# The modulation's accumulation steps moved from the neighbourhood projections to the queries, latent keys and values

## The chip, the cores and the metric

The kernel runs on one core of a Trainium2 chip. The metric is the device time in microseconds (us), the median of several executions. Five engines work side by side on queues of their own: TensorE (PE: matrix products into PSUM), VectorE (DVE), ScalarE (ACT), GpSimd (POOL) and SyncE (SP, which here issues the DMA loads). An instruction waits at the head of its engine's queue until what it needs is there, and everything queued behind it waits too.

## The reference, cut to what matters

One step of a diffusion backbone with two layers. In each layer 128 context tokens and 256 latent tokens (384 in three tiles of 128) go through a half-step feed-forward block, a block of three token mixers on the same input, and a second feed-forward block:

```
m  = split(silu(cvec) @ w_ada[l] + b_ada[l], 9)      # modulation, once for c_ctx and once for c
xp = ffn(modulate(xp, m[0], m[1]), gate m[2])
u_f, u_q, u_kv, k_rope, u_na = split(modulate(xp, m[3], m[4]) @ w_in)
y_f = fourier(u_f) @ w_branch_f
y_m = attention(query(u_q), keys and values of the latent kv) @ w_branch_m
y_n = neighbourhood_attention(q, k, v of u_na) @ w_branch_n
xp = xp + m[5] * ((sigmoid(h @ w_gate) * (y_f, y_m, y_n)) @ w_out)
xp = ffn(modulate(xp, m[6], m[7]), gate m[8])
```

The modulation is `silu(cvec) @ w_ada`: for each layer a matrix of 1024 x 9216 in fp32, read for two vectors only.

## The kernel before

All matrix products are fp32 values split into a high and a low part, three matmuls for one product: PE writes a result to one of eight PSUM banks, ACT writes the high part from the bank (a CAST), and DVE subtracts it for the low part (a TENSOR_TENSOR). The bank is free for a new result when both have read it. All PSUM tiles are taken from one pool in turn, so a new tile reuses the bank of the tile eight places earlier. Weights are split in the same way when loaded (`raw` into `whi` by ACT, `wlo` by DVE).

The modulation's matrix is not multiplied on PE. It is accumulated on DVE, a step at a time (`ada_step`): a step loads 128 rows x 1024 columns of `w_ada` (512 KB) and adds them, times one scalar per partition, to two accumulators `acc`, one for each vector. These are two SCALAR_TENSOR_TENSOR instructions; the first step of a block of eight has two TENSOR_SCALAR instead. After eight steps `ada_finish` transposes both accumulators (STREAM_TRANSPOSE, `at`) and reduces them (`red`), four DVE instructions more; three flushes later `ada_place` has one small matmul (`ada`, which takes a PSUM bank) and four small DVE instructions (`mod`), or for a gate block a write to DRAM.

Steps are issued by `ada_spend(n)` (L497), which takes n steps from the stage's budget, flushes what is due, and stops at a budget of zero:

```
budget = {(0, 0): 36, (0, 1): 12, (0, 2): 36, (1, 0): 36, (1, 1): 8, (1, 2): 0}
```

So layer 0's mixers spend 12 steps and layer 1's 8. In `mixer_body` the order of the code is: transposed queries and Fourier mixing, `query(t)` three times (tile `q`, `qtok`), the latent keys in four pairs (PSUM tile `kn`, results `k`), the latent values in four tiles (`v`, `vs`), the transposed heads (`qT`, `q`), eight chunks of the Fourier branch (`yb`, copied by DVE to `mg`), the latent attention, in whose fill the neighbourhood's values are projected (`nv`), then the neighbourhood's queries and keys (`nq`, `nk`, eight chunks), its attention, and the last branch. Before the change the steps stand with `nv` (three), ahead of `nq` (one) and with the `nq`/`nk` chunks (up to eight).

The order on PE, DVE and ACT is set by a scheduler from the order of the code and the dependences; SP keeps the order of the code. Loads are placed by a planner (`make_plan`, `place`), which gives each weight its moment from a clock of PE work and the free slots among 26 large buffers.

Of the kernel before, what the change touches and what calls it, by code (L numbers as in the profile page):

```python
# [88 lines left out]
class Kernel:  # L89
# [879 lines left out]
    def mixer_body(self, ph):  # L969
# [61 lines left out]
            ckT.append(kt)  # L1031

        def query(t):
            c = slice(t * P, (t + 1) * P)
            qk = self.slot([P, NH, HQ], F32, "qtok")
            for hh in range(2):
                b = self.psum("q")
                for kc in range(3):
                    w = self.W(("wuq", l, kc), "mla_w_uq", l, kc * P, 1, 0, 768)
                    self.mm3(b[:, 0:384], (qnT[kc][:, 0, c], qnT[kc][:, 1, c]),  # L1040
                             tuple(x[:, 0, hh * 384:hh * 384 + 384] for x in w), kc == 0, kc == 2)
                bv = b[:, 0:384].rearrange("p (h j) -> p h j", h=4)
                qs = qk[:, 4 * hh:4 * hh + 4]
                if t == 0:
                    nc.scalar.copy(out=qs, in_=bv)
                else:
                    nc.scalar.copy(out=qs[:, :, 0:64], in_=bv[:, :, 0:64])
                    self.rope(qs[:, :, 64:96], bv[:, :, 64:96], t - 1, 4)
            qtok.append(qk)

        for step, i in ((turn_q, 0), (turn_q, 1), (turn_q, 2), (four_tokens, 0), (four_tokens, 1), (four_tokens, 2), (four_tokens, 3),
                        (four_channels, 0), (turn_kv, 0), (turn_kv, 1), (query, 0), (four_channels, 1), (query, 1), (query, 2)):
            step(i)
# [7 lines left out]
        k96 = [self.slot([HQ, 2, 512], F32R, "k96") for _ in range(NH)]  # L1061
        w = self.ukv(l, 0)
        for pr in range(4):
            b = self.psum("kn")
            for kc in range(2):
                lhs = tuple(x[:, kc, 2 * pr:2 * pr + 2].rearrange("p a b -> p (a b)") for x in w)
                self.mm3(b, lhs, (ckT[kc][:, 0], ckT[kc][:, 1]), kc == 0, kc == 1)
            for e in range(2):
                kk = k96[2 * pr + e]
                self.split(kk[0:64, 0], kk[0:64, 1], b[64 * e:64 * e + 64, :])  # L1070
                nc.vector.tensor_copy(out=kk[64:96], in_=krt[64:96].bitcast(F32))
        w = self.ukv(l, 1)
        vm = []
        for t in range(4):
            b = self.psum("v")
            for kc in range(2):
                self.mm3(b, (ckT[kc][:, 0, t * P:(t + 1) * P], ckT[kc][:, 1, t * P:(t + 1) * P]),
                         tuple(x[:, kc].rearrange("p a b -> p (a b)") for x in w), kc == 0, kc == 1)
            vm.append(self.split_v(b))
# [494 lines left out]
```

## Time and profile before

| what | us |
|---|---|
| median of three runs | 1869.28 (1868.36 to 1870.4) |
| profiled execution | 1866.74 |
| its span, first to last instruction | 1865.0 |
| PE busy in it | 1842.9 |
| DVE busy in it | 1409.0 |

The profiled execution has its own time, 2.5 us under the median; stretches are read from it, and a change found in it is set on the median. Stretches are told in us from the span's start. Layer 0's queries, keys, values and Fourier branch lie between 353 and 395, its `nq` and `nk` between 471 and 506; layer 1's between 1273 and 1315 and between 1392 and 1426. An engine's idle time is shown in brackets with what ended it.

### The profile page before, as it was taken

What the parts mean: (1) busy time and instruction counts of PE and PEld (TensorE: products, weight loads), DVE (VectorE), ACT (ScalarE), POOL (GpSimd) and SP (SyncE); (2) the same over time, 40 slices, a digit from 0 to 9 for tenths busy, and PEclk for the clock granted to TensorE, in tenths of its full rate; (3) what the DMA queues carried; (4) which work ended last, traced back from release to release, by engine and by line L of the source; (5) the groups of instructions that cost most, each with busy time, mean ns of one, the idle gap of its engine ahead of it and who ended that gap; (6) DMA issues with size and microseconds to landing.
All of it is one profiled execution on the core that took longest, in us unless ns stands there. A gap on an engine that the chain in (4) does not pass through costs nothing. (4 is left out here: it accounts for less than half of the span.)

```text
span 1865.0 us, 27258 instructions
## 1 busy us (share of the span) xinstructions
PE 1842.9 (99%) x10568; PEld 1728.1 (93%) x10568; DVE 1409.0 (76%) x2206; ACT 785.3 (42%) x1305; POOL 94.7 (5%) x115
## 2 busy tenths in 40 slices
PE   8999999999999999999999999999999999999998
PEld 6899998999899999999999999989999998999997
DVE  6788888689997677888876888978798776533345
ACT  4433335556355453332453333355554553533330
POOL 0000002000100010000000000120001000000000
PEclk9999999999999999999999999999999999999999
DMA  9766656234835446666545666542356353444522
GB/s 325 264 224 212 206 209 207 88 102 126 234 109 188 125 148 221 196 226 219 188 159 186 221 220 219 193 157 89 113 177 183 104 190 130 133 135 125 145 92 79
DMA packets 225602, 320.22 MB, mean 172 GB/s; under 512 B 32784, under 2 KB 181888, under 8 KB 225344
## 3 DMA queue, kind: packets, MB, share of 16 engines
q1 hardware_dynamic: 223328, 313.88, 52.5%
q0 software_dynamic: 2112, 4.59, 0.6%
q8 instruction: 83, 1.36, 0.3%
q14 instruction: 47, 0.39, 0.1%
q10 hardware_dynamic: 32, 0.01, 0.0%
HBM read 312.32 MB, written 8.02 MB: 172 GB/s over the span
## 5 line engine op out<-in xcount | busy, mean ns | idle before, releaser
L193 DVE TENSOR_TENSOR wlo<-raw,whi 128x1024 fp32r<-128x1024 f32 (+4 forms) x420 | 488.7, 1181 | 148.7 <-ACT whi L188 68.0
L188 ACT CAST whi<-raw 128x1024 fp32r<-128x1024 f32 (+4 forms) x420 | 420.3, 1020 | 325.9 <-DVE wlo L193 83.7
L77 PE MATMUL w<-hmh,whi 128*128 128x384 f32 x1152 | 388.3, 337 | 0.8 <-ACT sl L77 0.8
L77 PE MATMUL w<-hmh,wlo 128*128 128x384 f32 x1152 | 387.1, 336 | 0.0
L77 PE MATMUL w<-hml,whi 128*128 128x384 f32 x1152 | 387.1, 336 | 0.0
L77 PE MATMUL y<-whi,sT 128*128 128x512 f32 x1050 | 335.1, 391 | 1.7 <-DVE sT L77 1.5
L77 DVE SCALAR_TENSOR_TENSOR acc<-raw,cs,acc 128x1024 f32<-128x1024 f32 x236 | 296.9, 1290 | 28.8 <-DMA raw<-in_w_ada_dram 28.5
L77 PEld LDWEIGHTS y<-whi,sT 128*128 128x128 f32 x1050 | 196.8, 188 | 41.1 <-DVE sT L77 2.1
L77 PEld LDWEIGHTS w<-hmh,whi 128*128 128x128 f32 x1152 | 216.6, 188 | 3.2 <-ACT sl L77 1.1
L77 PEld LDWEIGHTS w<-hml,whi 128*128 128x128 f32 x1152 | 216.6, 188 | 1.9
L77 PEld LDWEIGHTS w<-hmh,wlo 128*128 128x128 f32 x1152 | 216.6, 188 | 0.0
L77 PE MATMUL y<-wlo,sT 128*128 128x512 f32 x525 | 204.2, 389 | 0.0
L77 PE MATMUL g<-hmh,whi 128*128 128x384 f32 x384 | 132.5, 345 | 1.4 <-DVE qN L77 1.4
L77 PE MATMUL g<-hmh,wlo 128*128 128x384 f32 x384 | 129.8, 338 | 1.6 <-DVE wlo L193 1.6
L77 PE MATMUL g<-hml,whi 128*128 128x384 f32 x384 | 129.9, 338 | 0.0
L77 PEld LDWEIGHTS y<-wlo,sT 128*128 128x128 f32 x525 | 98.6, 188 | 18.1
L77 ACT CAST sT<-sl 128x384 fp32r<-128x384 f32 x72 | 37.1, 515 | 183.8 <-DVE sl L77 183.8
L77 PE MATMUL hd<-whi,hmh 128*128 128x256 f32 (+1 forms) x336 | 100.1, 300 | 1.6 <-ACT hmh L77 1.6
L77 PE MATMUL hd<-wlo,hmh 128*128 128x256 f32 (+1 forms) x336 | 99.0, 297 | 0.0
L77 PE MATMUL hd<-whi,hml 128*128 128x256 f32 (+1 forms) x336 | 98.9, 296 | 0.0
L77 ACT ACTIVATE sl<-w 128x384 f32<-128x384 f32 x72 | 35.4, 492 | 110.0 <-PE w L77 109.7
L77 POOL TENSOR_TENSOR st<-st,mhalf 128x1 f32<-128x1 f32 x48 | 43.9, 916 | 689.3 <-DVE st L77 689.2
(271 smaller groups left out, 2952.3 us busy)
## 6 DMA issues: line engine op xcount, KB each, us to landing
raw<-in_ffn_w_dram SPq DMA_DIRECT2D x244, 512.0 KB, 5.0
raw<-in_w_ada_dram SPq DMA_DIRECT2D x128, 512.0 KB, 4.9
raw<-in_w_gate_dram SPq DMA_DIRECT2D x48, 512.0 KB, 4.1
raw<-in_w_in_dram SPq DMA_DIRECT2D x32, 512.0 KB, 6.1
raw<-in_w_ada_dram SPq DMA_DIRECT2D x32, 256.0 KB, 5.9
raw<-in_w_out_dram SPq DMA_DIRECT2D x16, 512.0 KB, 6.8
raw<-gd SPq DMA_DIRECT2D x12, 512.0 KB, 5.1
raw<-in_ffn_w_dram SPq DMA_DIRECT2D x22, 256.0 KB, 5.8
```

Of the source, the lines that this page charges most:

```text
L77: r = f(*a, **kw)
L188: self.real.scalar.copy(out=hi, in_=r)
L193: self.real.vector.tensor_tensor(out=lo, in0=r, in1=hi.bitcast(F32), op=ALU.subtract)
```

## The change

Three lines are added in `mixer_body`: one step ahead of each of the three query tiles, one ahead of each of the four pairs of keys, and one ahead of every second of the four value tiles. The budgets stay, so each step spent here is one that the later calls no longer have.

```
         def query(t):
+            self.ada_spend(1)
             c = slice(t * P, (t + 1) * P)
...
         for pr in range(4):
+            self.ada_spend(1)
             b = self.psum("kn")
...
         for t in range(4):
+            self.ada_spend(t % 2)
             b = self.psum("v")
```

In layer 0 nine of the twelve steps are spent by these lines and three with `nv`; none is left for `nq` and `nk`. In layer 1 all eight are spent here. The accumulator's block ends inside the moved steps in both layers: in layer 0 with the first step of the keys, in layer 1 with the last step, at the values.

On DVE in layer 0, at the first two pairs of keys (`kn` is the pair's bank, `k` the split keys, `krt` the rotary part that is copied in). Before:

```order
L77 TENSOR_TENSOR k_648_3489<-kn_3497,k_648_3489 64x512
L77 CAST k_648_3489<-krt_3486 32x1024
L77 CAST k_649_3490<-krt_3486 32x1024
L77 TENSOR_TENSOR k_649_3490<-kn_3497,k_649_3490 64x512
L77 TENSOR_TENSOR k_650_3491<-kn_3512,k_650_3491 64x512
```

and now:

```order
L77 SCALAR_TENSOR_TENSOR acc_2385<-raw_3265,cs_161,acc_2385 128x1024
L77 TENSOR_TENSOR k_654_3507<-kn_3517,k_654_3507 64x512
L77 CAST k_654_3507<-krt_3504 32x1024
L77 CAST k_655_3508<-krt_3504 32x1024
L77 TENSOR_TENSOR k_655_3508<-kn_3517,k_655_3508 64x512
L77 STREAM_TRANSPOSE at_3531<-acc_2384 128x1024
L77 STREAM_TRANSPOSE at_3534<-acc_2385 128x1024
L77 TENSOR_REDUCE red_3530<-at_3531 128x32
L77 TENSOR_REDUCE red_3530<-at_3534 128x32
L77 TENSOR_SCALAR acc_3537<-raw_3292,cs_161 128x1024
L77 TENSOR_SCALAR acc_3538<-raw_3292,cs_161 128x1024
L77 TENSOR_TENSOR k_656_3509<-kn_3543,k_656_3509 64x512
```

Between the first pair's keys and the second's stand the end of one block and the first step of the next. Eight `acc` instructions (four steps) stand on DVE ahead of the first pair in both layers: two steps between the split of the last `uq` weights and the low part of `f`, the third among the transposed queries and the Fourier products, and the two halves of the fourth ahead of the second Fourier chunk and ahead of the first key. Behind that, layer 0 has a step after the second and after the third pair, and one behind the first and one behind the third value tile; layer 1 has a step after each of the first three pairs, one behind the first value tile, and the block's end behind the second.

On PE in layer 0, where the last pair of keys gives way to the first value tile. Before:

```order
L77 MATMUL kn_3542<-ckT_3348,whi_3310 128x512 x2
L77 MATMUL kn_3542<-ckT_3348,wlo_3311 128x512
L77 MATMUL v_3555<-whi_3397,ckT_3338 128x512
L77 MATMUL v_3555<-wlo_3398,ckT_3338 128x512
L77 MATMUL v_3555<-whi_3397,ckT_3348 128x512
```

and now:

```order
L77 MATMUL kn_3579<-ckT_3360,whi_3322 128x512 x2
L77 MATMUL kn_3579<-ckT_3360,wlo_3323 128x512
L77 MATMUL ada_3594<-red_3530,quad_105 128x64
L77 MATMUL v_3601<-whi_3415,ckT_3352 128x512
L77 MATMUL v_3601<-wlo_3416,ckT_3352 128x512
```

The small matmul on `red` stands in front of the values and takes a bank, so that the tiles behind it reuse banks one place earlier: the first `yb` chunk has the bank of the fourth pair of keys, where before it had the third's.

On DVE in layer 0, at the first `nq` and `nk` chunks. Before:

```order
L77 SCALAR_TENSOR_TENSOR acc_4668<-raw_4583,cs_161,acc_4668 128x1024
L77 SCALAR_TENSOR_TENSOR acc_4669<-raw_4583,cs_161,acc_4669 128x1024
L193 TENSOR_TENSOR wlo_4709<-raw_4619,whi_4708 128x1024
L193 TENSOR_TENSOR wlo_4727<-raw_4621,whi_4726 128x1024
L77 TENSOR_TENSOR kN_4739<-nk_4704,kN_4739 128x384
L77 TENSOR_TENSOR kN_4739<-cnkT_4655,kN_4739 128x128
L77 COPY kf_4660<-nk_4704 128x128
L77 SCALAR_TENSOR_TENSOR acc_4668<-raw_4593,cs_161,acc_4668 128x1024
L77 SCALAR_TENSOR_TENSOR acc_4669<-raw_4593,cs_161,acc_4669 128x1024
```

and now:

```order
L77 SCALAR_TENSOR_TENSOR qN_4739<-nq_4714,qN_4739 128x384
L193 TENSOR_TENSOR wlo_4747<-raw_4641,whi_4746 128x1024
L193 TENSOR_TENSOR wlo_4765<-raw_4644,whi_4764 128x1024
L77 TENSOR_TENSOR kN_4779<-cnkT_4708,kN_4779 128x128
L77 TENSOR_TENSOR mod_3596<-ada_4785,bad_107 32x16 x3
L77 TENSOR_TENSOR kN_4779<-nk_4742,kN_4779 128x384
L77 COPY kf_4713<-nk_4742 128x128
```

No `acc` instruction is left there; the end of the second block stands just ahead of these rows.

## Rows read from the trace of the kernel before

**Rows 1.** The page's first part: engine, busy us (share of the span), instructions.

```profile
PE 1842.9 (99%) x10568; PEld 1728.1 (93%) x10568; DVE 1409.0 (76%) x2206; ACT 785.3 (42%) x1305; POOL 94.7 (5%) x115
```

**Rows 2.** Stretches: length, then busy PE, PEld, DVE, ACT, POOL; PE clock, DMA share, GB/s.

```profile
353.00:365.00 12.00, 12.00 (x74) 11.96 (x73) 11.38 (x35) 8.22 (x17) 0.00 (x0) 1.00 0.00 1
365.00:376.00 11.00, 11.00 (x52) 9.17 (x51) 9.99 (x22) 5.64 (x10) 0.00 (x0) 1.00 0.00 1
376.00:392.00 16.00, 15.57 (x90) 14.88 (x90) 14.62 (x22) 8.79 (x13) 0.00 (x0) 1.00 0.34 104
392.00:440.00 48.00, 48.00 (x316) 47.81 (x315) 37.93 (x85) 29.32 (x71) 0.00 (x0) 1.00 0.29 87
...
510.00:515.00 5.00, 4.18 (x15) 4.18 (x16) 5.00 (x7) 0.27 (x1) 2.48 (x1) 0.66 0.26 85
...
1426.00:1515.00 89.00, 89.00 (x590) 88.14 (x587) 67.83 (x174) 50.67 (x109) 2.43 (x2) 1.00 0.42 137
```

**Rows 3.** Waits of PE in the mixers: total us, times, longest us.

```profile
PE yb L77 <- DVE k L77: 0.4, 1, 0.4
...
PE g L77 <- DVE wlo L193: 1.6, 1, 1.6
PE g L77 <- DVE qN L77: 1.4, 1, 1.4
```

**Rows 4.** Timeline of PE in layer 0: start, us, instruction [idle before, releaser].

```profile
380.06 0.59 PE L77 MATMUL yb<-oF,whi 128*128 128x384 f32 x2 [0.43 <-DVE k L77]
```

**Rows 5.** Timeline of DVE in layer 0, from the last kv norm to the values.

```profile
344.74 0.48 DVE L77 SCALAR_TENSOR_TENSOR ckv<-kv,st,raw 128x256 f32<-128x256 f32 x1 [0.73 <-POOL st L77]
...
348.31 0.69 DVE L77 TENSOR_TENSOR f<-uf,f 128x512 fp32r<-128x512 f32 x1 [2.60 <-ACT f L77]
...
351.35 0.57 DVE L77 TENSOR_TENSOR gl<-fa,gh 128x392 fp32r<-128x392 f32 x1 [0.48 <-ACT gh L77]
...
365.75 0.29 DVE L77 TENSOR_TENSOR qtok<-q,rp 128x128 f32<-128x128 f32 x1 [0.62 <-ACT qtok L77]
...
379.22 0.69 DVE L77 TENSOR_TENSOR k<-kn,k 64x512 fp32r<-64x512 f32 x1
...
381.69 1.88 DVE L77 TENSOR_TENSOR vs<-v,vs 128x512 fp32r<-128x512 f32 x3
```

**Rows 6.** Timeline of DVE in layer 0, at the first `nk` chunk: a block's end and steps.

```profile
479.63 1.21 DVE L77 TENSOR_REDUCE red<-at 128x32 f32<-128x1024 f32 x1
480.76 1.24 DVE L77 STREAM_TRANSPOSE at<-acc 128x1024 f32<-128x1024 f32 x1
481.92 0.71 DVE L77 TENSOR_SCALAR acc<-raw,cs 128x1024 f32<-128x1024 f32 x1
...
484.33 2.48 DVE L77 SCALAR_TENSOR_TENSOR acc<-raw,cs,acc 128x1024 f32<-128x1024 f32 x2
486.73 2.35 DVE L193 TENSOR_TENSOR wlo<-raw,whi 128x1024 fp32r<-128x1024 f32 x2
```

**Rows 7.** The chain that ended last, layer 1: start, us, engine and what.

```profile
1299.28 0.68 DVE k L77
...
1300.10 14.80 PE yb L77 x84
```

**Rows 8.** Timeline of DVE in layer 1, the second to fourth value tiles.

```profile
1301.72 1.88 DVE L77 TENSOR_TENSOR vs<-v,vs 128x512 fp32r<-128x512 f32 x3
```

**Rows 9.** Timeline of PE in layer 0, behind the neighbourhood's first scores.

```profile
510.82 0.45 PE L77 MATMUL g<-hmh,wlo 128*128 128x384 f32 x1 [1.64 <-DVE wlo L193]
...
511.31 0.52 PE L77 MATMUL g<-hml,whi 128*128 128x384 f32 x1
...
514.20 0.52 PE L77 MATMUL g<-hml,whi 128*128 128x384 f32 x1
```

**Rows 10.** The page's DMA issues: count, KB each, median us from issue to landing.

```profile
raw<-in_w_ada_dram SPq DMA_DIRECT2D x128, 512.0 KB, 4.9
```

More of the change, by code (lines that the diff above doesn't have):

```diff
@@ L1033, in query @@
         def query(t):
+            self.ada_spend(1)
             c = slice(t * P, (t + 1) * P)
@@ L1063, in mixer_body @@
         for pr in range(4):
+            self.ada_spend(1)
             b = self.psum("kn")
@@ L1074, in mixer_body @@
         for t in range(4):
+            self.ada_spend(t % 2)
             b = self.psum("v")
```

## The prediction

> **What bounds the kernel now.** I read the page's first part, then stretches of the mixers, then PE's waits, then the timelines. Over the whole span PE is busy 99% and DVE 76% [rows 1], which looks as if DVE had room everywhere. The stretches say otherwise. Where the steps go, DVE is the fuller engine: 11.38 of 12 us, 9.99 of 11 and 14.62 of 16 from 353 to 392 [rows 2]. PE still shows no idle time there because it runs ahead of DVE on its eight banks. How much of that lead is left is shown by the one wait in this stage: the second `yb` chunk waits 0.4 us for DVE's last keys, in layer 0 at 380.06 (the same row stands once more in layer 1) [rows 3, 4]. The lead is used up. Whatever delays DVE's keys now delays PE by as much.
>
> The Trainium skill (Perfetto Trace Analysis, Identifying the Most-Contended Engine) ranks engines by occupancy. By that ranking over the span, PE alone binds, DVE work is free, and the result is the third rival's. The same page (Optimization Strategy) lets the contended engine change with the regime; the stretches and the 0.4 us wait agree with that half.
>
> Where the steps came from, PE loses something in layer 0 alone. Its first gate chunk behind the scores waits 1.4 us for DVE's `qN` and 1.6 us for a `wlo` [rows 3], and after that the granted clock is 0.66 in a stretch of 5 us [rows 2]: ten matmuls start 0.32 us apart from 511.31 to 514.20 [rows 9] against 14.80 us for 84, 0.176 each, at the full 2.4 GHz [rows 7]. Ten times 0.145 is 1.4 us. In layer 1 PE is busy in every microsecond from 1426 to 1515 [rows 2].
>
> **The change, part by part.**
>
> *Removed.* Layer 0's `nq`/`nk` lose nine steps' worth of DVE time, so I take all three losses as gone: 1.4 + 1.6 + 1.4 = 4.4 us. The block's end that still stands there (four instructions) is hidden under chunks on which PE never waited before. Layer 1 gains nothing, since PE had no wait there.
>
> *Prices on DVE.* Two SCALAR_TENSOR_TENSOR in a row hold DVE from 484.33 to 486.73: a step costs 2.40 us, an instruction 1.20. A transpose takes 480.76 to 481.92, 1.16, and a reduction 479.63 to 480.76, 1.13; a block's end is two of each, 4.58. From 481.92 to 484.33 are two TENSOR_SCALAR and one reduction, so a block's first step is 2.41 - 1.13 = 1.28 [rows 6].
>
> *Added ahead of the first keys, both layers.* Eight `acc` instructions, 9.60 us. What absorbs them is DVE's idle time in that stretch: 0.73 before `ckv` and 2.60 before the low part of `f`, then five short waits for ACT from 0.48 (at 351.35) to 0.62 (at 365.75), 2.22 together [rows 5]. That is 5.55. ACT and POOL, on which these waits hung, keep their times, so a later DVE finds them done. DVE reaches the first keys 9.60 - 5.55 = 4.05 us late. The same order stands in layer 1, with the same idle times to 0.1 us, so I use 4.05 twice.
>
> *Layer 0 from there.* The block's end, 4.58, a first step, 1.28, and two steps, 4.80, come before the last keys: 4.05 + 4.58 + 1.28 + 4.80 = 14.7 us late. The last keys ended at 379.22 + 0.69 = 379.9 [rows 5], now 394.6. Because the `ada` matmul took a bank, the first `yb` chunk waits for exactly these keys. From 394.7 eight chunks take 8/7 of 14.80, 16.9 us, to 411.6; before, seven of them ran from 380.06 [rows 4] to 394.9. PE is 16.8 us late. The two steps among the values do not add to this: the second value tile ends at about 382.3 + 14.7 + 3.1 (a step and the small `mod` instructions) = 400.1 against 401.0, when PE comes to the chunk that takes its bank, and the fourth at 383.6 + 14.7 + 5.5 = 403.8 against 405.3 [rows 5].
>
> *Layer 1.* Three steps lie between the first and the last keys: 4.05 + 7.20 = 11.3, so the second `yb` chunk starts at 1311.4 instead of 1300.1 [rows 7]. One more step and the block's end come before the third value tile, which ended at 1303.0 (two thirds through 1.88 us from 1301.72 [rows 8]) and now ends 4.05 + 9.60 + 4.58 = 18.2 later, at 1321.2. The fifth chunk takes its bank; four chunks, 8.4 us, end at 1329.6, against 1314.9 before [rows 7]. PE is 14.7 us late.
>
> *Is it given back?* DVE's lag is worked off under `yb`, but PE's is not: it is busy 48.00 of 48 us from 392 to 440 [rows 2], so nothing behind the delay can shrink.
>
> *Clock.* Each layer now has long waits of PE among the keys and values. Before, 3.0 us of waits were followed by a half-speed stretch that cost 1.4 [rows 9]. Inside the stretch that DVE sets, slow matmuls cost nothing; behind the last wait they do. I take 1.4 once a layer, 2.8, between 0 and one drop for each of three long waits a layer, 8.4.
>
> *Loads.* Nine loads of `w_ada` now stand in SP's queue among those of `w_ukv` and `w_branch_f` and ahead of `w_gate`. DMA is idle from 353 to 376 (share 0.00) [rows 2], a load lands in 4.9 us [rows 10], and most of the new ones only wait for buffers that PE frees in the `uq`, `kv` and `uf` projections. I cost them at nothing; if that cover fails, DVE waits one landing in each layer, 9.8 us.
>
> *Sum.* 16.8 + 14.7 - 4.4 + 2.8 = 29.9 us. The profiled execution, 1866.74, becomes 1896.6; the median, 1869.28, becomes 1899.2, which is the forecast.
>
> **The rivals.**
>
> *The clock keeps dropping.* PE's work in the two stages falls into short bursts between waits, and the half speed reaches into chunks that PE sets. For it: the drop came after only two waits [rows 9]. Against it: only the last burst of each layer lies on the path. Six drops of 1.4 instead of two: 1904.8. The Trainium skill (TensorE: Matmul & The Clock Gate, A second HAM failure mode: psum-queue depth-cycling) describes a kernel whose small waits while cycling through banks sent the clock back and forth at a cost in throughput. By that account this rival holds; the trace has one drop and cannot decide.
>
> *Loads come late.* One landing more in each layer, 9.8 us: 1909.0. For it: branch and gate weights now wait for buffers that the moved steps release, so their loads start later. Against it: the empty DMA before.
>
> *DVE has room after all.* The steps hide behind PE, and only the gain is left: 1869.28 - 4.4 = 1864.9. It decides if PE's lead on the banks, measured where `yb` begins, is larger than the 15 us by which DVE falls back; the wait there says that the lead is 0. For it speaks only the 76% over the span.
>
> *A draw.* The lead covers all but some 4 us, which the gain cancels: 1869.3. It needs the same hidden lead.
>
> That the change does not do what it says is excluded by the order: no `acc` row is left in the projections.
>
> **How the numbers follow.** Forecast 0.66, clock 0.14, late loads 0.12, room on DVE 0.05, draw 0.03. The forecast's own lower bound is no clock loss, -2.8, and as much idle absorbed again as I counted, -11.1: 1885. Its upper bound, no idle absorbed, +11.1, gives 1910, and the late loads end at 1909. I take 1885 to 1911; outside lie the two cases around no change, 0.08, and some of the combined mishaps. A measurement of this kernel can tell about 0.2%, 3.7 us, from no change. Faster 0.05, same 0.03, slower 0.92.
>
> **What would show it.** In the changed profile PE should wait for DVE in layer 0 at the `ada` matmul, at a `qT` transpose and at the first `yb` chunk, some 17 us together, and in layer 1 at the transposes, the first two `yb` chunks and the fifth, some 15; DVE should be busy without a gap from `f` to the Fourier branch; the clock should fall below 1 near 395 and 1321; the `g` waits of 1.4 and 1.6 should be gone; `acc` should never wait for its load. The forecast is wrong if PE's idle time in the two stages is under 10 us, if DVE shows gaps there that end on a DMA, or if layer 0's `g` waits stay.

## The result, and the profile after

The changed kernel takes 1895.49 us (median of 4 runs, 1893.84 to 1895.88) against 1868.82 for the kernel before in the same session: a ratio of 1.0142, 95% interval 1.0124 to 1.0159, so 26.5 us slower (23.2 to 29.7). The forecast was 1899.2 in a range of 1885 to 1911. The profiled execution took 1895.4 us, its span 1893.6.

The page after, for [rows 1]: busy time, then the PE clock in 40 slices of the span.

```profile
PE 1851.7 (98%) x10568; PEld 1734.4 (92%) x10568; DVE 1405.3 (74%) x2206; ACT 784.9 (41%) x1305; POOL 94.3 (5%) x115
...
PEclk8999999989999999999999999998999999999999
```

The two 8s behind the start are the slices with the two mixers' key and value stages. The stretches there, to be read against [rows 2]: length, then busy PE, PEld, DVE, ACT, POOL, the PE clock, the DMA share, GB/s.

```profile
353.00:365.00 12.00, 11.69 (x77) 11.39 (x77) 12.00 (x23) 8.29 (x15) 0.00 (x0) 1.00 0.47 180
365.00:376.00 11.00, 9.88 (x51) 8.52 (x50) 10.86 (x36) 4.54 (x10) 0.00 (x0) 1.00 0.07 23
376.00:412.00 36.00, 24.33 (x108) 22.20 (x109) 34.97 (x46) 11.43 (x17) 0.00 (x0) 0.81 0.25 75
412.00:460.00 48.00, 48.00 (x317) 47.81 (x316) 38.38 (x86) 29.12 (x71) 0.00 (x0) 1.00 0.37 111
520.00:540.00 20.00, 20.00 (x124) 19.68 (x124) 12.98 (x37) 9.14 (x21) 0.00 (x0) 1.00 0.45 127
```

DVE fills every stretch up to 412 and PE stands for 11.7 of 36 us. From 520 to 540, where the neighbourhood's first scores and gate chunks lie now, PE is busy throughout at full clock; before, it waited for `qN` and `wlo` at this place, 508 to 511 [rows 3, 9].

Waits of PE after, in layer 0 from 335 to 420: total us, times, longest us.

```profile
PE ada L77 <- DVE red L77: 6.2, 1, 6.2
PE yb L77 <- DVE k L77: 4.6, 1, 4.6
PE qT L77 <- DVE k L77: 2.0, 1, 2.0
PE fa L77 <- DVE f L77: 0.7, 1, 0.7
PE fo L77 <- DVE gl L77: 0.3, 1, 0.3
```

And in layer 1, from 1250 to 1350:

```profile
PE yb L77 <- DVE k L77: 6.7, 2, 5.8
PE yb L77 <- DVE vs L77: 1.7, 1, 1.7
PE qT L77 <- DVE k L77: 1.1, 1, 1.1
...
```

Every one is on DVE, none on a load, and DVE itself waits for no load in these stages. The places are those that the prediction named, and two that it did not: `fa` and `fo` wait for DVE's part of `f` and `gl`, which is late too (0.7 and 0.3 us in each layer).

To add up layers and kernels I use marks on PE's timeline: the first `fa` matmul, where the Fourier branch begins, the first score `s` behind the `yb` chunks, and the first `nq` of layer 0. First the kernel before, then the changed one; columns are start, us, instruction.

```profile
348.40 0.36 PE L77 MATMUL fa<-whi,f 128*128 128x260 f32 x1
...
394.72 1.50 PE L77 MATMUL s<-k,q 96*128 96x384 f32 x9
...
471.86 0.42 PE L77 MATMUL nq<-hmh,whi 128*128 128x384 f32 x1
...
1268.41 0.36 PE L77 MATMUL fa<-whi,f 128*128 128x260 f32 x1
...
1314.73 1.50 PE L77 MATMUL s<-k,q 96*128 96x384 f32 x9
```

```profile
350.63 0.36 PE L77 MATMUL fa<-whi,f 128*128 128x260 f32 x1
...
415.50 1.50 PE L77 MATMUL s<-k,q 96*128 96x384 f32 x9
...
492.63 0.42 PE L77 MATMUL nq<-hmh,whi 128*128 128x384 f32 x1
...
1282.74 0.36 PE L77 MATMUL fa<-whi,f 128*128 128x260 f32 x1
...
1343.58 1.50 PE L77 MATMUL s<-k,q 96*128 96x384 f32 x9
```

From `fa` to `s` was 46.32 us in both layers. It is now 64.87 in layer 0 (+18.55) and 60.84 in layer 1 (+14.52). From the first `nq` of layer 0 to layer 1's `fa`, where the time is given back, it was 796.55 and is 790.11 (-6.44). The sum is +26.6, the measured difference. The 2.2 us by which `fa` starts later than before arose in the first 40 us, ahead of the change (granted clock over the first 100 us: 0.95 against 0.98). In the profiled executions of all kernels below, this start lies anywhere between 348.2 and 351.6, at 349.9 in one that moves no step ahead of it, so it is no part of the change.

The delay has two parts. Between the marks, first in the kernel before (layer 0, layer 1), then in the changed one:

```profile
348.40:394.72 46.32, 45.89 (x267) 43.30 (x266) 41.28 (x85) 25.94 (x46) 0.00 (x0) 1.00 0.19 62
1268.41:1314.73 46.32, 45.92 (x267) 43.33 (x266) 41.28 (x85) 25.94 (x46) 0.00 (x0) 1.00 0.19 62
```

```profile
350.63:415.50 64.87, 51.11 (x270) 47.12 (x268) 63.24 (x109) 25.88 (x45) 0.00 (x0) 0.89 0.32 108
1282.74:1343.58 60.84, 50.34 (x267) 46.61 (x266) 60.01 (x102) 27.85 (x47) 0.00 (x0) 0.89 0.32 107
```

PE stands 13.8 and 10.5 us, less than the 17 and 15 that the prediction named as signs. The rest is work at half clock: PE is busy 5.2 and 4.4 us longer with all but the same matmuls, at a granted clock of 0.89. Most of this slow work lies ahead of another wait for DVE, which takes it in.

### The profile page after: what moved, and what is told of

Its sections match the earlier page's. It is cut to its first block, busy times and chain, and to the rows that moved or that the text cites. A ratio compares the mean times of both kernels' runs of the same rounds, so it can differ in the third digit from the quotient of the medians.

```text
span 1893.6 us, 27247 instructions
## 1 busy us (share of the span) xinstructions
PE 1851.7 (98%) x10568; PEld 1734.4 (92%) x10568; DVE 1405.3 (74%) x2206; ACT 784.9 (41%) x1305; POOL 94.3 (5%) x115
```

## The experiments

All kernels were timed against the kernel before. The marks give each stage's time in the profiled execution, in us. Added up, the marks of a kernel differ from its time by up to 3.7 us: the time holds each execution's start as well, and the kernel before was profiled 2 to 3 us below its median. So differences of a few us are read from the marks.

| kernel | time against before (95%) | layer 0, `fa` to `s` | layer 1, `fa` to `s` | `nq` to layer 1's `fa` |
|---|---|---|---|---|
| before | | 46.32 | 46.32 | 796.55 |
| changed | +26.5 (23.2 to 29.7) | 64.87 | 60.84 | 790.11 |
| layer 0 alone | +8.8 (6.5 to 11.2) | 64.72 | 46.32 | 789.97 |
| layer 1 alone | +13.6 (11.0 to 16.3) | 46.32 | 62.44 | 796.05 |
| half the accumulation | +10.1 (7.3 to 12.9) | 58.27 | 52.59 | 790.58 |
| block's end held back | +19.3 (16.5 to 22.1) | 62.11 | 57.85 | 790.17 |
| `ada` matmul late | +22.1 (19.1 to 24.9) | 62.48 | 60.88 | 791.34 |
| block boundary moved | +28.0 (24.5 to 31.6) | 66.08 | 60.88 | 790.20 |
| casts on POOL | +18.5 (15.7 to 21.5) | 61.25 | 59.14 | 790.97 |
| query steps alone | -0.7 (-2.8 to +1.1) | 47.74 | 47.73 | 793.02 |
| steps spread later | -2.6 (-4.3 to -0.7) | 46.32 | 46.30 | 794.15 |
| two early steps, rest spread | -4.3 (-6.2 to -2.6) | 47.13 | 46.30 | 792.17 |

**One layer at a time.** Against the changed kernel, at each of the three added places, as for the queries (and `l == 1` for layer 1 alone):

```diff
         def query(t):
-            self.ada_spend(1)
+            if l == 0:
+                self.ada_spend(1)
```

> Only the first layer's mixer spends its steps with queries, keys and values; the second layer's stand where they stood before. My theory (DVE is full in this stage and PE's lead on the eight banks is used up, so PE is late by what DVE's keys and values are late, each layer for itself): the first layer's part of the sum alone, 16.8 + 1.4 for the clock - 4.4 = +13.8 us over the kernel before; with the changed kernel's trace (18.4 late at the end of the yb chunks, about 6.2 less afterwards) +12. PE waits of some 17 us between queries and first yb chunk in layer 0, none over 0.4 us in layer 1's keys and values. Rival (the moved loads shift the whole queue of weights, so the loss belongs to the run and not to the layer): not the sum of its parts, at least +18. Rival (half-speed clock carries the loss): 0 to +3 per layer once PE's waits are taken off.

> Only the second layer's mixer spends its steps with queries, keys and values. My theory: layer 1 had no loss to give back where the steps came from, so all of its lag stands: +14.7 by the prediction's sum, +14.4 by the changed kernel's trace; layer 0 keeps its 1.4 and 1.6 us waits of the gate chunks. This and the other layer's kernel add up to the whole change, about +26.6. Rival (loads): together clearly more or less than +26.6, or DVE waits for w_ada.

In time, layer 0 alone is a miss: +8.8, with an interval that ends below the +12 expected. +8.8 and +13.6 make 22.4, which is 4.1 less than the whole change; taken together, the three intervals allow about 5, so the times neither show nor exclude that the parts add up. By the marks they do: 18.40 - 6.58 = 11.8 for layer 0, 16.12 - 0.50 = 15.6 for layer 1, together 27.4. The other layer's stage is 46.32 in both, as before, so each layer's loss stays in its layer, and it is layer 0 that gets time back (6.58 against 0.50). The loss does not belong to the queue of loads.

**Half the accumulation.**

```diff
-        for cd in range(2):
+        for cd in range(1 if self.hold and k else 2):
             a, sc = self.acc[cd], self.cs[:, k, cd:cd + 1]
```

`hold` is set from the queries to the last value tile. There the kernel leaves out the second vector's accumulation, except in a block's first step.

> As the changed kernel, but of the moved steps' two acc instructions the second is left out (except in a block's first step), in both layers; so the gates and modulations that come from it are wrong. Loads, the block's end, the ada matmul and its bank stay. My theory (DVE's work in the stage is the price): ahead of the first keys 4 instructions, 4.8 us, less than the 5.55 idle, so 0 late; layer 0's last keys are 4.58 + 1.28 + 2.4 = 8.3 late and PE, behind the bank of the ada matmul, some 10.4 + 1.4 for the clock; layer 1's third value tile is 4.58 + 4 x 1.2 = 9.4 late, which the four chunks ahead of the fifth nearly cover: PE 3.6 to 4.0 late. With 4.4 to 6.2 given back in layer 0: +9 to +12 us over before. Rival (late loads or the ada matmul's bank are the price): the loads are the same, so near +26. Rival (time goes with the count of acc instructions in proportion): 9/17 of +26.6, +14.

+10.1, where the loads are those of the changed kernel (their buffers come free earlier, though). The interval ends at 12.9, which excludes the +26 of the rival with the loads and, narrowly, the +14 of the one in proportion. Layer 0 came out to the term: DVE's first key starts at 367.94, 19.59 behind `fa` (before 367.79, 19.39), so 4.8 us were absorbed all but 0.2; its last key ends at 388.25, 8.4 late (expected 8.3); PE is 11.95 late (expected 11.8). Layer 1 was a miss: 6.3 instead of 3.6 to 4.0. The third value tile was late as reckoned and the fifth `yb` chunk waited 2.2 us for it; I had written that the four chunks ahead nearly cover this, without working it out.

**The bank of the `ada` matmul.** The steps and the block's end on DVE stay; only the matmul goes behind the values.

```diff
-        self.ada_due.append([3, lambda: self.ada_place(blk, red)])
+        self.ada_due.append([9 if self.hold else 3, lambda: self.ada_place(blk, red)])
```

> As the changed kernel, but in the mixers the ada matmul comes six places later, behind the values in layer 0; the block's end on DVE (transposes and reductions) stays where it was, and so do all steps. My theory (the ada matmul takes one bank, so that the first yb chunk and not the second waits for the last keys): the last keys stay 14.9 us late, the wait moves to the second yb chunk and the first chunk, 2.1 us, runs ahead of it: 16.4 us late at the scores of layer 0 instead of 18.5; layer 1 within 1.6 us of the changed kernel's 14.5. About -2 against the changed kernel, +24 to +25 over before. Rival (PE loses the 6.2 us that it stands at the ada matmul): 6 us less, +20.

Layer 0 takes 62.48, 16.16 late (expected 16.4), and layer 1 60.88. In time +22.1, with an interval that overlaps that of the changed kernel, so the trace has to decide. PE's timeline in layer 0, waits in brackets:

```profile
384.61 0.85 PE L77 MATMUL qT<-ident,qtok 128*96 128x128 f32 x3 [4.57 <-DVE k L77]
...
390.89 0.98 PE L77 MATMUL yb<-oF,whi 128*128 128x384 f32 x2 [5.43 <-DVE k L77]
...
396.03 0.98 PE L77 MATMUL yb<-oF,whi 128*128 128x384 f32 x2 [0.96 <-DVE k L77]
```

The 6.2 us at the `ada` matmul are gone, and all but 1.8 us of them come back at `qT` and the first two chunks: the wait sits where the next bank is missing. The last keys now hold up the second chunk, and one chunk's time is saved. Of the 2.4 us gained in this stage about 0.5 are not the bank's: the last keys end at 395.88, 45.87 behind `fa`, 14.4 late instead of 14.9. The 6.2 us as such were no loss of their own.

**The block's end, two ways.** First, `ada_flush` does not start a block's end while `hold` is set:

```diff
-        if self.ada_fin:
+        if self.ada_fin and not self.hold:
             self.ada_fin.pop(0)()
```

> As the changed kernel, but the block's end that falls among keys and values (two transposes, two reductions, then the ada matmul) is held back until the first value tile of the neighbourhood, under the attention. My theory: in layer 0 the last keys are 4.05 + 1.28 + 4.80 = 10.1 late instead of 14.7, and the second yb chunk, not the first, waits for them: PE 10.1 late instead of 16.8, 6.7 less; in layer 1 the third value tile is 4.58 earlier, so the fifth chunk does not wait: 11.3 instead of 14.7, 3.4 less. Together 10 us less than the changed kernel: +16 to +17 over before, if the block's end finds cover in the attention, and +26 again if it doesn't (then PE waits behind the attention's tiles). Rival (loads, clock): within 3 us of the changed kernel.

+19.3, less than the changed kernel but some 3 us more than expected. Layer 1 is 11.5 late, as reckoned (11.3). Layer 0 is 15.8 late instead of 10.1, although its last keys are only 8.1 late (they end at 390.25, 39.61 behind `fa`); its waits are new ones. PE's timeline there, and then ACT's:

```profile
389.83 1.65 PE L77 MATMUL yb<-oF,whi 128*128 128x384 f32 x4 [8.83 <-ACT whi L188]
```

```profile
388.25 0.58 ACT L77 CAST k<-kn 64x512 fp32r<-64x512 f32 x1 [3.96 <-DVE k L77]
388.73 1.04 ACT L188 CAST whi<-raw 128x1024 fp32r<-128x1024 f32 x1
```

PE waits for the split of branch weights, 8.83 us here and 2.38 us at 399. The high part that the first chunk waits for stands in ACT's order behind a key's cast, which waits for DVE. A late load is not the reason: SP's queue did stand 28.9 us at one load, for a buffer that an `acc` instruction releases, but that load was issued at 387.5, too late for this split (loads of this stretch land 4.3 us after their issue at the earliest), and all before it had been issued by 358.2. The block that is held keeps its two `acc` buffers while the next one takes two more, from the same pool as the weights. That this moved the loads and splits is argued from the planner's code, not shown. So this kernel tested two things at once in layer 0.

Second, the block boundary is shifted instead, and no buffer is held longer for it:

```diff
-        budget = {(0, 0): 36, (0, 1): 12,
+        budget = {(0, 0): 32, (0, 1): 16,
```

> As the changed kernel, but the first feed-forward spends 32 steps instead of 36 and the first mixer 16 instead of 12, so that in layer 0 a block begins with the queries and ends behind the second value tile, as in layer 1; no buffer is held longer for it. My theory (in layer 0 the block's end ahead of the last keys and the bank of its ada matmul make the first yb chunk wait for them): first keys 1.28 + 7.2 - 5.55 = 2.9 late, last keys 10.1 late instead of 14.7, the second yb chunk waits for them and the fifth for the third value tile (2.9 + 9.6 + 4.58 = 17.1 late); PE 13 to 15 late in layer 0, as it is in layer 1, instead of 18.4. So 4 to 5 us less than the changed kernel, +21 to +23 over before, if three more steps in the projections cost nothing, up to 3 more if they bring the g waits back. Rival (the place of the block's end does not matter, only the work): within 1.5 us of the changed kernel.

A miss: +28.0 (66.08 in layer 0), no faster than the changed kernel. PE waits where expected (the second `yb` chunk for the last keys, 0.97 us; the fifth for the third value tile, 1.82 us), but the first keys are late already: 378.28 is 26.72 behind `fa`, 7.3 us late and not 2.9. DVE's timeline shows why:

```profile
351.48 0.69 DVE L77 TENSOR_TENSOR f<-uf,f 128x512 fp32r<-128x512 f32 x1 [2.61 <-ACT f L77]
...
361.39 1.41 DVE L77 TENSOR_SCALAR acc<-raw,cs 128x1024 f32<-128x1024 f32 x2
362.71 1.28 DVE L77 SCALAR_TENSOR_TENSOR acc<-raw,cs,acc 128x1024 f32<-128x1024 f32 x1
```

The first accumulation of a new block stands ten microseconds behind `f` in DVE's order, and the 2.61 us ahead of `f` stay idle. Of the 5.55 us of idle time counted in the prediction, 0.9 us are used here. The 4.4 us lost this way are what the later block's end saved.

**DVE relieved from the other side.**

```diff
-                nc.vector.tensor_copy(out=kk[64:96], in_=krt[64:96].bitcast(F32))
+                nc.gpsimd.tensor_copy(out=kk[64:96], in_=krt[64:96].bitcast(F32))
```

> As the changed kernel, but the eight copies of the rotary part into each layer's keys (CAST, 0.65 us each on DVE) stand on POOL, which has nothing to do there. Nothing that waits for DVE's accumulations or for a load is altered. My theory (DVE's time in the stage is what PE waits for): last keys 5.2 us earlier in each layer, PE too: some 10 us less than the changed kernel, +16 over before. If ACT, which writes the other half of the keys, is next, less: 5 us less, +21. Rival (loads, or PE's own stops for bank and clock, set the end): no change from +26. Rival (POOL's work slows DVE's beside it): DVE's key and acc instructions longer than 0.69 and 1.20, and the gain smaller by as much.

8 us less than the changed kernel in time, but 3.6 and 1.7 in the two stages: the direction of my theory, but not the size. The last keys of layer 0 are 12.1 late instead of 14.9. The last rival explains part of the difference. DVE in layer 1, then POOL over the same stretch:

```profile
1300.64 2.06 DVE L77 SCALAR_TENSOR_TENSOR acc<-raw,cs,acc 128x1024 f32<-128x1024 f32 x1
...
1310.53 2.05 DVE L193 TENSOR_TENSOR wlo<-raw,whi 128x1024 fp32r<-128x1024 f32 x1
```

```profile
1300.53 14.92 POOL L77 CAST k<-krt 32x1024 fp32r<-32x1024 f32 x8 [24.10 <-DVE krt L77]
```

Beside POOL's casts an `acc` took up to 2.06 us instead of 1.28 and a weight split 2.05 instead of 1.21. The order explains another part: one more `acc` stands ahead of the last keys in each layer than in the changed kernel. DVE does not wait for ACT at the keys, so ACT is not what comes next.

**How much is free.** Against the changed kernel, only the queries' spending is kept:

```diff
         for pr in range(4):
-            self.ada_spend(1)
             b = self.psum("kn")
```

and the same at the values.

> Of the move only the three query steps of each layer are kept; keys and values spend nothing, and what is left of the budget goes to the value tiles of the neighbourhood and its projections, as before. My theory (idle time of DVE ahead of the first keys absorbs the first 5.55 us): 6 instructions, 7.2 us, less 5.55 leave the first and the last keys 1.65 us late in each layer and PE as much, 3.3 together, with 0 to 1.5 for the clock; against it stands what layer 0 gets back, anything from nothing to the 6.4 us that the trace of the changed kernel shows, since five of eight steps stay there. So -3 to +3 us over before. Rival (each moved step costs its share): 6 of 17 steps of +26.6, +9.4.

No change that can be measured. The stages are 1.42 and 1.41 us longer where 1.65 was expected, while 6 of 17 steps in proportion would have been +9.4. So of 7.2 us of accumulation 5.8 cost nothing. Layer 0 gets 3.5 us back, although PE now waits 2.3 us for weights of the first `nk`.

**What the old place cost, without the loss.** From the kernel before, steps leave the neighbourhood's query projections for the branch pieces of its attention:

```diff
             for nme in ("nq", "nk"):
-                self.ada_spend(1)
+                if nme == "nk":
+                    self.ada_spend(1)
...
+                if x == 1:
+                    self.ada_spend(1)
                 g = early.pop(d) if d in early and x == 2 else self.gate_chunk(l, x, d)
```

> The kernel before, with every second step of the neighbourhood's projections (the one ahead of each query projection) moved to the first branch pieces in the neighbourhood's attention instead, in layer 0 alone, since layer 1's budget ends sooner; queries, keys and values spend nothing. My theory (what the change removes is worth 4.4 us by the prediction, 6.4 by the changed kernel's trace, and it can be had without the loss, as DVE has 18 us of room between 525 and 620): -4 to -6 us under before; no g wait on qN or wlo, no half clock near 511. Rival (the steps then hold up the pieces' g and ptl tiles): the waits only move, 0 to +3.

-2.6 us. The waits for `qN` and `wlo` are gone, but two gate chunks now wait 2.2 us for DVE's `g`; both expectations were partly right. The next kernel also puts two steps into layer 0's first queries (`if l == 0 and t < 2: self.ada_spend(1)`) and only the rest (`d > 1`) under the pieces.

> The kernel before, with two steps in layer 0's first two queries and none in layer 1's, one step at each key projection of the neighbourhood (none at the query projections) and the remaining two under the first branch pieces. In the order of DVE the four accumulations stand ahead of the low part of f. My theory (only DVE's idle time ahead of f is free, 5.55 us of it counted in the prediction): 4.8 us are absorbed whole, the stage from f to the scores takes what it took before (46.3 us from the first fa to the first s), and layer 0 gives back 3 to 6 us behind the projections: -3 to -6 us against before. Rival (any accumulation in this stage delays the keys): 4.8 us later at the scores, so 0 to +2.

-4.3 us (2.6 to 6.2): 1864.31 against 1869.0, faster than both kernels. Layer 0 gives back 4.38 us, although PE now waits 1.5 us for a weight of the first `nk`. The four added accumulations all stand ahead of `f`:

```profile
347.50 2.48 DVE L77 SCALAR_TENSOR_TENSOR acc<-raw,cs,acc 128x1024 f32<-128x1024 f32 x2
349.89 0.69 DVE L77 TENSOR_TENSOR f<-uf,f 128x512 fp32r<-128x512 f32 x1
```

The stage is 0.8 us longer, not 0: `f`, which began 0.1 us ahead of the first `fa` before, begins 1.6 behind it, and PE waits 0.7 us for it. The idle time ahead of `f` alone is 3.3 us, less than these 4.8; the rest of the 5.55 lies behind `f`.

## Why the prediction was right, and where its terms were off

**The bound.** Right. DVE was the full engine and PE's lead on the banks was used up: work added on DVE came out at PE in full beyond the idle time (query steps alone, half the accumulation). The Trainium skill (Perfetto Trace Analysis, Identifying the Most-Contended Engine) ranks engines by occupancy (TensorE by its weight loads, here 93%); by the share over the span (DVE 76% before) this change would be free. The stretch decided, as that page's sentence on regimes (Optimization Strategy) allows.

**Ahead of the first keys.** Forecast 4.05 late; the first key after starts at 373.68, 23.05 behind `fa` against 19.39 before: 3.7. Two small errors cancel in part: from 8 us ahead of `fa` to the first key, DVE is 8.9 us busier, not 9.60, and 5.25 of 5.78 us of idle time are gone, not 5.55 (0.44 of the 0.73 ahead of `ckv` stays). That this much was absorbed is because half of the accumulations stood ahead of `f`, with its 2.60 us of idle time, in DVE's order. That was read from the order, but not named as a condition; the shifted boundary showed that it is one.

**Layer 0.** Forecast: last keys 14.7 late, first `yb` chunk behind them, 16.8 and 1.4 for the clock. DVE's timeline after, and then PE's:

```profile
391.21 0.69 DVE L77 TENSOR_TENSOR k<-kn,k 64x512 fp32r<-64x512 f32 x1 [0.68 <-ACT k L77]
...
396.36 0.69 DVE L77 TENSOR_TENSOR k<-kn,k 64x512 fp32r<-64x512 f32 x1
```

```profile
381.04 0.66 PE L77 MATMUL ada<-red,quad 128*128 128x64 f32 x2 [6.16 <-DVE red L77]
...
392.05 0.50 PE L77 MATMUL qT<-ident,qtok 128*96 128x128 f32 x3 [1.99 <-DVE k L77]
...
397.19 0.98 PE L77 MATMUL yb<-oF,whi 128*128 128x384 f32 x2 [4.64 <-DVE k L77]
```

The last keys end at 397.05, 46.42 behind `fa` against 31.51: 14.9 late, 0.7 of it a wait for ACT that was not foreseen ("DVE busy without a gap" was wrong by this one gap). The first chunk starts at 397.19, and `s` follows 18.31 later: 16.9 for eight chunks and 1.4 for the clock. PE is 18.55 late by the marks, where 18.2 was forecast. The late `ada` matmul confirmed the bank.

**Layer 1.** Forecast 14.7 and 1.4 for the clock; measured 14.52. PE's timeline, and then DVE's at the third value tile:

```profile
1320.09 0.98 PE L77 MATMUL yb<-oF,whi 128*128 128x384 f32 x2 [5.78 <-DVE k L77]
...
1325.23 0.98 PE L77 MATMUL yb<-oF,whi 128*128 128x384 f32 x2 [0.97 <-DVE k L77]
...
1335.18 0.59 PE L77 MATMUL yb<-oF,whi 128*128 128x384 f32 x2 [1.73 <-DVE vs L77]
```

```profile
1334.36 1.28 DVE L77 TENSOR_TENSOR vs<-v,vs 128x512 fp32r<-128x512 f32 x2
```

The fifth chunk waits for the third value tile as forecast, and four chunks take 8.40 us behind it. The clock term of 1.4 failed here: the half speed that begins at 1320 ends ahead of the fifth chunk, and the wait there takes it in.

**Given back.** Forecast 4.4, measured 6.44: the mis-sized term. Beside the two `g` waits, 3.0, also a wait of 0.4 for `oT` and 0.8 of one for `sT` went, in layer 0's attention and the feed-forward behind it, which the prediction did not list. The half-clock stretch is worth more than the ten matmuls that I counted: a granted clock of 0.91 over 20 us is 1.8 us (an estimate, taking all of it as lost). The stretch before:

```profile
500.00:520.00 20.00, 16.96 (x96) 16.27 (x95) 20.00 (x38) 7.54 (x16) 8.37 (x6) 0.91 0.53 144
```

That makes 6.0; the last 0.4 is not traced.

So the sum of 29.9 was 3.3 too high: 2.0 by what was given back, 1.4 by layer 1's clock, 0.2 by the rest of layer 1, less the 0.35 that was missing in layer 0.

**The rivals.** Late loads: excluded for this change by the waits of PE and DVE in these stages, none of which ends on a load, and by the half accumulation. In the kernel that held two more buffers one load was issued late, but PE's long waits there do not hang on it. The clock that keeps dropping: it did fall at nearly every long wait of these stages (0.81 over 36 us), but most of that lies in front of another wait. The Trainium skill (TensorE: Matmul & The Clock Gate, A second HAM failure mode: psum-queue depth-cycling) describes such a clock with a loss of throughput; the trace agrees on the clock, and the loss here was 1.4 us, since DVE set the pace. Room on DVE and the draw are excluded by the 26.5 us.

## What to carry to other kernels

An engine's room is read from the stretch in which the work is to go, and there as idle time that lies behind the added instructions in that engine's order, ahead of the next result that the leading engine waits for. Up to that time work is free, beyond it each microsecond counted here. One short wait of the leading engine on a buffer (0.4 us here) was the sign that its lead was used up. When waits move from one buffer to the next as something is taken away, none of them is the loss; the loss is set by the chain of the slow engine and by which chunk needs its last result. Half-clock work ahead of another wait was covered by that wait, and counted only where nothing waited behind it.

## What was not expected of the hardware

After like waits the clock did not always do the same. In the changed kernel the fifth chunk of layer 1 ran at 2.4 GHz behind waits of 5.78, 0.97 and 1.73 us; with layer 1 alone, behind much the same waits of 5.77, 0.96 and 1.94 us, it fell back to 1.2 GHz. The clock over this chunk in the changed kernel, and then with layer 1 alone (columns as above):

```profile
1335.00:1337.00 2.00, 1.82 (x11) 1.85 (x12) 2.00 (x5) 0.35 (x1) 0.00 (x0) 1.00 0.72 212
```

```profile
1319.00:1321.00 2.00, 0.89 (x3) 0.92 (x4) 2.00 (x5) 1.35 (x2) 0.00 (x0) 0.82 0.23 61
1321.00:1323.00 2.00, 2.00 (x8) 2.00 (x8) 2.00 (x4) 0.00 (x0) 0.00 (x0) 0.50 0.69 234
```

Four chunks then took 9.99 us, not 8.40. So one such wait ahead of work that PE sets costs 0 or 1.6 us; why the one or the other is open.

A small copy on POOL lengthened some of DVE's instructions: at most from 1.28 to 2.06 us for an accumulation (the others beside the casts in layer 1 took 1.33 or 1.34) and from 1.21 to 2.05 for a split. The keys' low parts, which read one input from a bank, kept their 0.69. The Trainium skill (SBUF — State Buffer, Terms) says that DVE and GpSimd hold a pair of ports in turn, the other blocking for a whole instruction; the two long rows agree with a DVE instruction that waits behind a cast; that they did is not shown.
